# Layer 1: latent products and gates ahead of the spatial gating, whose products run ahead of group 2's state-space input product

## The chip, the cores and the metric

The kernel runs on one core of a Trainium2 chip. The metric is the time of one execution on the device in microseconds (us); lower is better. The kernel before takes 1910.93 us (median of three runs, 1908.58 to 1912.76).

The core's engines work side by side, each through its own queue in order: PE (TensorE, matrix products), DVE (VectorE), ACT (ScalarE), POOL (GpSimd), and SP, which issues the DMAs here.

## The reference

A two-layer block over 512 latent tokens and 256 context tokens of width 1024. In each layer the normalised, modulated input h goes through one input projection that is split into four mixers; their outputs are joined, projected and added; then comes a feed-forward with a convolution. Cut to what matters here:

```
def layer(x, c):                          # x: 512 latent tokens, c: 256 context tokens
    h = rmsnorm(x) * (1 + scale) + shift  # both streams
    p = h @ w_in                          # columns for A, B, C, D
    A: u, v = split(gelu(p_A));  v = rmsnorm(v) by heads;  out = u * (w_sp @ v + b_sp)
    B: q, k, v, r, gl = split(p_B); gate = cumsum(log_sigmoid(gl @ w_gate + b) / 16)
       out = rmsnorm(chunked gated linear attention(q, k, v, gate)) * silu(r)
    C: out = s5(p_C)                      # u -> complex state scan, both directions -> y
       y = gelu(y);  out = y * sigmoid(y @ w_glu + b_glu)
    D: latent attention on rmsnorm(p_D[:224]) (q) and rmsnorm(p_D[224:320]) (k, v), rotary
    x = x + gate * rmsnorm(concat(A, B, C, D) @ w_out)
    x = x + gate * rmsnorm(conv_ffn(rmsnorm(x) * ...))
```

In layer 1, the last, the context stream is read but not written: the outputs are the latent tokens.

## The kernel before

Tokens are worked in three groups of 256: groups 0 and 1 are the latent tokens, group 2 the context. h lies in SBUF as high and low parts (hhx and hlx for groups 0 and 1, hh2 and hl2 for group 2), and each weight tile, 128 x 1024, is loaded (`raw`, 512 KB, four buffers) and split into whi (ACT, L191) and wlo (DVE, L192), three buffers each. A product takes three matmuls for each of eight slices: `mm3` (L199, L200, L201).

The order on each engine is not written out: the scheduler of the tile framework simulates the program (`schedule_with_timeline_sim=True`) and lays down a fixed order from the order in which the code opens tiles and from its own times; pools and their tags (PSUM banks above all) decide what must wait for what. PSUM tags that matter: `pf` (six banks of the feed-forward, which stays open into the norm that ends a layer), `pn` (norms), `pg` (two banks for the mixers' input products), `pc1` (S5), `pb2` (one buffer, two banks) and `pb1` (mixer B, mixer A and the latent norms).

The place of the change is the passage from layer 0 to layer 1. At the end of layer 0's feed-forward a norm chain runs for each group: squares on ACT and DVE, sums by PE (`sums`, L322), root on DVE and POOL (L124, L125), broadcast by PE (`bcast`, L145), and `modulate`, which writes hh and hl by ACT, DVE and POOL (L385 to L391). Woven into it run the units of layer 1's S5 input product: `c_units` returns four units for groups 0 and 1, and two late units for group 2, which share the two weight tiles; each ends in a copy from PSUM to `rawm` (L1228). Then `mixers` runs for layer 1:

- `mixer_c` (S5): it transposes rawm into `s5a` (L696) and `s5u` (L703), multiplies by E (L714), copies into the state `s5v` (DVE L722 for one direction, ACT L724 for the other), and scans on DVE: seven steps over 12 blocks, eleven steps from block to block (L735, L737, L738 each), and a correction of all blocks (L753, L760, L762, L763). The states are copied to H (ACT L776, DVE L774), multiplied (L786, L788), put through gelu (L792), transposed (L798), gated (L814, L816 to L818) and stored.
- products ua and va of mixer A (in `pg`; ua has 48 matmuls of 512 columns, va 96 of 256), then `mixer_a`: squares and norm of va (L990, L991, L995), the spatial product (L1001, in `pb2`), L1003 and L1005, whose result `ut` is stored to DRAM.
- products cq and ck of mixer D, and the first part of `mixer_b`, the gates of four heads, in two pairs: L845 (PE, in `pb2`), L848 (ACT, Abs) and L849 (DVE); then for each pair Exp and Ln (ACT, L851, L852, each with a table load); then L855, L856 (a scan), L858, L859, L860 on DVE; last `dec` (DVE L866, L867 and ACT L868).
- `latent_norms`: squares (ACT L1037), sums (PE L1039, in `pb1`), root, broadcast (L145, in `pb2`), L1054 on DVE.
- product q (evacuated into tile `x12`, where `ut` and va were; L1536), its scaling L873 and L874, product vb (L1623), then k (L1536), r and the rest of `mixer_b` and `mixer_d`.

The scheduler merges these strands, so on PE the S5 instructions stand among the products.

Of the kernel before, what the change touches and what calls it, by code (L numbers as in the profile page):

```python
# [14 lines left out]
AF = mybir.ActivationFunctionType  # L15
ALU = mybir.AluOpType
AX = mybir.AxisListType
PSUM = bass.MemoryType.PSUM
# [4 lines left out]
T = NX + NCX  # L23
# [67 lines left out]
class Net:  # L91
# [1218 lines left out]
    def run(self, out):  # L1310
# [77 lines left out]
        for l in range(L):  # L1388
            ctx = l < L - 1
            G = (0, 1, 2) if ctx else (0, 1)  # L1390
            tn = T if ctx else NX
            self.mixers(l, ctx, md, (psls, tabs, tables) if l == 0 else None)
            with self.pool("f") as fp, self.pool("psf", space=PSUM) as psp:
# [43 lines left out]
                with ExitStack() as ye:  # L1437
# [60 lines left out]
                    if ctx:  # L1498
                        uf = [self.t(self.wp, [128, D], "rawm", bufs=2)[:, :T] for _ in range(2)]
                        self.uf[l + 1] = uf  # L1500
                        cu, late = self.c_units(l + 1, uf, psp)
                        self.weave(WV[4], down[1], c[:1])
                        self.weave(WV[5], down[2] + cu[:2], c[:2])
                        self.weave(WV[6], cu[2:], c[1:])
                        self.weave("", late, [])
                    else:
                        self.weave(WV[7], down[1], c)
            xsrc = xd
        es.close()

    def mixers(self, l, ctx, md, early=None):
# [9 lines left out]
        def fm(wv, groups):  # L1521
            px = pc = None
            if 0 in groups:
                px = self.t(self.psg, [128, 512], "pg")
                self.gemm_fm(wv, KT, self.hrhs, px, None, [g for g in groups if g < 2])
            if 2 in groups:
                pc = self.t(self.psg, [128, 512], "pg")
                self.gemm_fm(wv, KT, self.hrhs, None, pc[:, :256], [2])
            return px, pc


        def half(n, i):
            return self.wsplit(l, ("in", n), i)
# [6 lines left out]
        def tmajor(name, groups, sink):  # L1540
            wvs = [half(name, q) for q in range(2)]
            for g in groups:
                ps = self.t(self.psg, [128, 512], "pg")
# [9 lines left out]

        psls, tabs, tables = early or (self.pool("psb", space=PSUM), None, None)
# [5 lines left out]
        self.psg = psgs.__enter__()  # L1560
        mxs = self.pool("mx")
        px_ = mxs.__enter__()
        env = SimpleNamespace()
# [10 lines left out]
        rest = iter(())  # L1574

        def visit(n):
            for _ in range(n):
                next(rest, None)

        with self.pool("mc") as pm:  # L1580
# [7 lines left out]
            x12 = self.t(px_, [128, 4, T], "x12")  # L1588
            x6 = self.t(px_, [128, 1536], "x6")
            ut = x12[:, 0:2]  # L1590
            va = x12[:, 2:4].rearrange("p a t -> p (a t)").rearrange("p (i c) -> p i c", i=6)
            for i in range(2):
                px, pc = fm(half("ua", i), G)
                evac(ut[:, i], px, pc, func=AF.Gelu_apprx_tanh)
                visit(1)
            tmajor("va", G, lambda g, ps: nc.scalar.activation(
                va[:, 2 * g:2 * g + 2].rearrange("p i c -> p (i c)"), ps[:], AF.Gelu_apprx_tanh))
# [5 lines left out]
            for i in range(2):  # L1603
                px, pc = fm(half("cq", i), G3 if i else G)
                evac(cq[:, i], px, pc)
                visit(1)
            px, pc = fm(half("ck", 0), G3)
            evac(ck, px, pc)
            visit(2)
            if tabs:  # L1610
                tabs.__exit__(None, None, None)
            mgs = self.pool("mg", side="right")
            pg = mgs.__enter__()
            b = self.mixer_b(l, env, cq[:, 1], pg, ("pb2", "pb1"), ctx)
            next(b)
# [191 lines left out]
```

## Time and profile before

| | |
|---|---|
| median of three runs | 1910.93 us (1908.58 to 1912.76) |
| the profiled execution | 1912.24 us; its span 1910.4 us |
| PE busy | 1775.8 us, 93% of the span |
| DVE, ACT, POOL busy | 1197.7 us (63%), 776.7 us (41%), 123.9 us (6%) |
| TensorE's granted clock, mean | 0.944 of 2.4 GHz |
| chain that ended last | PE 71%, DVE 11%, issue 9%, ACT 4%, DMA 2% |

Busy time is that of one execution, taken by the hardware profiler; ends of matmuls are modelled, so for the rate of products the distance between two starts is read, not the length of one. The names L12 are lines of the kernel before. An idle time in brackets is the time that the engine waited ahead of an instruction, with the instruction that let it go on. The rows are in a section of their own below.

### The profile page before, as it was taken

The numbers are of one execution on the slowest core, as the hardware profiler recorded it, in microseconds if no ns is written. First come the engines' busy times: TensorE is split into PE (matmuls) and PEld (weight loads), VectorE is DVE, ScalarE is ACT, GpSimd is POOL, SyncE is SP. The second block draws the span as 40 slices with busy tenths as digits, with TensorE's granted clock in tenths as the row PEclk, the third lists the DMA queues.
The fourth block names the chain that finished last, engine by engine and source line by source line (L and its number), as shares of the span: only waits on it lengthen the run. The fifth ranks groups of instructions, "written<-read, shape, count | busy, mean of one in ns | idle before, by whom it ended". The sixth has DMA issues, their size and how long they took to land.

```text
span 1910.4 us, 28205 instructions
## 1 busy us (share of the span) xinstructions
PE 1775.8 (93%) x11256; PEld 1515.4 (79%) x11256; DVE 1197.7 (63%) x2200; ACT 776.7 (41%) x1242; POOL 123.9 (6%) x142
## 2 busy tenths in 40 slices
PE   5899989899989899999999988997989999999996
PEld 2785677679977788888888886886668988888886
DVE  8866734664879853554885775683565765455555
ACT  2433454454753333322322344364444653333332
POOL 0000000000430000000000033000000310000002
PEclk7999998899999999999999988998889899999998
DMA  9457630015623342222564433323102523323341
GB/s 351 140 170 253 200 95 24 28 37 185 204 70 112 109 122 78 88 89 85 183 185 133 143 100 104 115 69 95 33 24 94 187 83 88 110 78 110 86 146 45
DMA packets 94386, 222.14 MB, mean 116 GB/s; under 512 B 10928, under 2 KB 41008, under 8 KB 93232
## 3 DMA queue, kind: packets, MB, share of 16 engines
q1 hardware_dynamic: 94256, 220.36, 37.0%
q8 instruction: 88, 1.44, 0.3%
q14 instruction: 42, 0.34, 0.1%
HBM read 193.35 MB, written 24.08 MB: 114 GB/s over the span
## 4 chain that ended last, share of the span: by engine, by line
PE 71%; DVE 11%; issue 9%; ACT 4%; DMA 2%; POOL 1%; SPq 0%; POOLq 0%; DVEq 0%; ACTq 0%
PE pf L199 16%; PE pf L200 16%; PE pf L201 16%; PE pg L199 3%; PE pg L201 3%; PE pg L200 3%; PE pb L243 1%; DVE wlo L192 1%; PE pd L1161 1%; PE pn L322 1%; DVE z L1215 1%; PE pc L714 1%; ACT whi L191 1%; DMA bk<-bk 1%; DVE nu L389 1%
## 5 line engine op out<-in xcount | busy, mean ns | idle before, releaser
L192 DVE TENSOR_TENSOR wlo<-raw,whi 128x1024 fp32r<-128x1024 f32 (+1 forms) x215 | 252.5, 1175 | 292.4 <-ACT whi L191 289.5
L191 ACT ACTIVATE whi<-raw 128x1024 fp32r<-128x1024 f32 (+1 forms) x215 | 217.4, 1011 | 398.0 <-PE pf L200 340.7
L199 PE MATMUL pf<-hhx,whi 128*128 128x512 f32 (+1 forms) x1032 | 365.8, 360 | 13.3 <-DVE z L1215 6.0
L200 PE MATMUL pf<-hlx,whi 128*128 128x512 f32 (+1 forms) x1032 | 369.1, 359 | 6.1 <-DVE hlx L391 5.9
L201 PE MATMUL pf<-hhx,wlo 128*128 128x512 f32 (+1 forms) x1032 | 366.8, 357 | 0.7 <-DVE wlo L192 0.5
L199 PEld LDWEIGHTS pf<-hhx,whi 128*128 128x128 f32 x1032 | 199.9, 196 | 41.2 <-issue 7.3
L200 PEld LDWEIGHTS pf<-hlx,whi 128*128 128x128 f32 x1032 | 201.8, 196 | 33.6 <-DVE hlx L391 8.9
L201 PEld LDWEIGHTS pf<-hhx,wlo 128*128 128x128 f32 x1032 | 201.8, 196 | 27.0 <-DVE wlo L192 1.5
L199 PE MATMUL pf<-g,whi 128*128 128x512 f32 (+1 forms) x552 | 185.8, 342 | 5.3 <-DVE z L1215 2.9
L201 PE MATMUL pf<-g,wlo 128*128 128x512 f32 (+1 forms) x552 | 187.5, 341 | 0.8 <-DVE wlo L192 0.8
L200 PE MATMUL pf<-g,whi 128*128 128x512 f32 (+1 forms) x552 | 187.8, 341 | 0.0
L1215 DVE SCALAR_TENSOR_TENSOR z<-pf,cols,z 128x511 f32<-128x511 f32 (+1 forms) x264 | 167.9, 656 | 28.3 <-ACT z L1213 25.8
L200 PE MATMUL pf<-hl,whi 128*128 128x256 f32 x432 | 123.0, 286 | 0.4 <-DVE hl L391 0.4
L199 PE MATMUL pf<-hh,whi 128*128 128x256 f32 x432 | 121.5, 286 | 1.6 <-ACT hh L390 1.5
L201 PE MATMUL pf<-hh,wlo 128*128 128x256 f32 x432 | 122.1, 284 | 0.0
L199 PEld LDWEIGHTS pf<-g,whi 128*128 128x128 f32 x552 | 104.7, 192 | 18.8 <-issue 3.7
L201 PEld LDWEIGHTS pf<-g,wlo 128*128 128x128 f32 x552 | 105.8, 192 | 12.2 <-DVE wlo L192 1.0
L200 PEld LDWEIGHTS pf<-g,whi 128*128 128x128 f32 x552 | 105.8, 192 | 11.5 <-DVE g L1265 0.2
L1213 ACT ACTIVATE z<-pf,cols 128x512 f32<-128x512 f32 (+1 forms) x132 | 90.1, 695 | 38.3 <-PE pf L201 29.9
L1294 DVE TENSOR_TENSOR y<-y,pf 128x512 f32<-128x512 f32 (+1 forms) x88 | 44.7, 515 | 73.1 <-PE pf L201 73.1
L125 POOL TENSOR_TENSOR nroy<-nroy,mhalf 128x2 f32<-128x2 f32 x10 | 10.0, 996 | 1202.4 <-DVE nroy L124 894.3
L199 PEld LDWEIGHTS pf<-hh,whi 128*128 128x128 f32 x432 | 82.4, 193 | 3.9 <-ACT hh L390 2.3
(465 smaller groups left out, 3408.5 us busy)
## 6 DMA issues: line engine op xcount, KB each, us to landing
raw<-in_w SPq DMA_DIRECT2D x170, 512.0 KB, 3.5
rawm<-in_wmod SPq DMA_DIRECT2D x64, 512.0 KB, 4.3
raw<-in_w SPq DMA_DIRECT2D x48, 384.0 KB, 3.2
wm<-in_wmod SPq DMA_DIRECT2D x8, 1024.0 KB, 10.4
silu<-in_wmod SPq DMA_DIRECT2D x16, 512.0 KB, 5.6
dx<-g SPq DMA_DIRECT2D x32, 256.0 KB, 2.3
dG<-gt SPq DMA_DIRECT2D x16, 256.0 KB, 2.8
dE<-es SPq DMA_DIRECT2D x16, 256.0 KB, 2.3
```

Of the source, the lines that this page charges most:

```text
L191: nc.scalar.activation(hv, src, AF.Copy)
L192: nc.vector.tensor_tensor(lv, src, hv.bitcast(F32), op=ALU.subtract)
L199: self.nc.tensor.matmul(out, lh, rh, start=i == 0, stop=False)
L200: self.nc.tensor.matmul(out, lh, rl, start=False, stop=False)
L201: self.nc.tensor.matmul(out, ll, rh, start=False, stop=i == n - 1)
L243: self.nc.tensor.matmul(acc[32 * q:32 * q + 2, :], self.ct[:, k, :], halves[q // 2][:, q % 2 * 512:q % 2 * 512 + 512], start=k == 0, stop= ...
L322: self.nc.tensor.matmul(ps[:, j:j + 1], acc[:, k, j * 128:(j + 1) * 128], self.ones[:, 0:1], start=k == 0, stop=k == 1)
L389: nc.vector.scalar_tensor_tensor(u[:], xk, sc, pb, op0=ALU.mult, op1=ALU.mult)
L714: nc.tensor.matmul(ps[:, g * NCH:(g + 1) * NCH], E[:, b * 4 + g, :], U[:, gg, :], start=True, stop=True)
L1213: nc.scalar.activation(z[:, o:o + m], p[:, :m], AF.Identity, bias=b, scale=w1)
L1215: self.last = nc.vector.scalar_tensor_tensor(z[:, o + d:o + d + m - 1], p[:, s:s + m - 1], w, z[:, o + d:o + d + m - 1], op0=ALU.mult, op1 ...
L1294: nc.vector.tensor_tensor(y[:, m, t0:t0 + tw], y[:, m, t0:t0 + tw], ps[:, :tw], op=ALU.add)
```

## The change

Three things are moved, in layer 1 alone. The feed-forward's PSUM pool now stays open past the end of layer 0, and `mixers` gets it with the late units. First, products va and ua run in `pf` banks ahead of the late units (group 2's S5 input product). Second, `c_units` is called twice, once for the four early units and once for the two late ones, so that the late ones load and split the two weight tiles again. Third, `latents` (products cq and ck, and mixer_b's first part) comes ahead of `mixer_a`. In layer 0 all stands in the old order.

```diff
@@ run
+            if l == 0:
+                self.mixers(l, ctx, md, early=(psls, tabs, tables))
+            else:
+                self.mixers(l, ctx, md, late=(psf, psp, late))
+            psf = self.pool("psf", space=PSUM)
+            psp = psf.__enter__()
+            with self.pool("f") as fp:
...
-                        cu, late = self.c_units(l + 1, uf, psp)
+                        cu = self.c_units(l + 1, uf, psp)[0]
+                        late = self.c_units(l + 1, uf, psp)[1]
                         self.weave(WV[6], cu[2:], c[1:])
-                        self.weave("", late, [])
@@ mixers
+        def va_product():
+            tmajor("va", G, lambda g, ps: nc.scalar.activation(
+                va[:, 2 * g:2 * g + 2].rearrange("p i c -> p (i c)"), ps[:], AF.Gelu_apprx_tanh))
+        def ua_product():
+            for i in range(2):
+                px, pc = fm(half("ua", i), G)
+                evac(ut[:, i], px, pc, func=AF.Gelu_apprx_tanh)
+                visit(1)
+        if late:
+            psf, psp, units = late
+            self.psg = psp, "pf"
+            va_product()
+            ua_product()
+            for u in units:
+                u()
+            psf.__exit__(None, None, None)
...
+            def latents():
+                for i in range(2):
+                    px, pc = fm(half("cq", i), G3 if i else G)
+                    evac(cq[:, i], px, pc)
+                    visit(1)
+                px, pc = fm(half("ck", 0), G3)
+                evac(ck, px, pc)
+                visit(2)
+                if tabs:
+                    tabs.__exit__(None, None, None)
+                mgs = self.pool("mg", side="right")
+                pg = mgs.__enter__()
+                b = self.mixer_b(l, env, cq[:, 1], pg, ("pb2", "pb1"), ctx)
+                next(b)
+                return mgs, pg, b
+            if l:
+                mgs, pg, b = latents()
+            if not late:
+                ua_product()
+                va_product()
             visit(2)
             self.mixer_a(l, ut, va, x6, px_, "pb2", ctx)
             visit(2)
             for k in range(2):
                 store(0, k, ut[:, k])
+            if l == 0:
+                mgs, pg, b = latents()
```

The lists below show what stands in a row on an engine. PE at the end of layer 0's last norm, before (tile pf: products of the S5 input; pg: the first of ua's; hhx and hlx: groups 0 and 1, hh_1528 and hl_1529: group 2):

```order
L201 MATMUL pf_10525<-hhx_3543,wlo_10409 128x256
L322 MATMUL pn_10595<-ones_70,nsa_10563 128x1 x4
L145 MATMUL pn_10595<-cst_68,nry_10600 128x128 x2
L199 MATMUL pf_10647<-hh_1528_10605,whi_10376 128x256
L199 MATMUL pf_10673<-hh_1528_10605,whi_10408 128x256
...
L201 MATMUL pf_10673<-hh_1528_10605,wlo_10409 128x256
L696 MATMUL pc_1553_10750<-cst_68,rawm_9958 96x128
...
L696 MATMUL pc_1554_10756<-cst_68,rawm_9959 96x128
L199 MATMUL pg_11093<-hhx_3543,whi_11089 128x512
```

The same place now (pf_10672 and pf_10722: va; pf_10778 and pf_10810: ua; pf_10842 and pf_10874: group 2's S5 input; pg_11281: cq):

```order
L201 MATMUL pf_10672<-whi_10662,hlx_3544 128x256
L322 MATMUL pn_10595<-ones_70,nsa_10563 128x1 x4
L199 MATMUL pf_10672<-whi_10668,hhx_3543 128x256
...
L145 MATMUL pn_10595<-cst_68,nry_10600 128x128 x2
...
L199 MATMUL pf_10778<-hhx_3543,whi_10774 128x512
...
L201 MATMUL pf_10810<-hhx_3543,wlo_10807 128x512
L199 MATMUL pf_10842<-hh_1528_10605,whi_10838 128x256
...
L201 MATMUL pf_10874<-hh_1528_10605,wlo_10871 128x256
L696 MATMUL pc_1577_10940<-cst_68,rawm_9958 96x128
...
L696 MATMUL pc_1578_10946<-cst_68,rawm_9959 96x128
L199 MATMUL pg_11281<-hhx_3543,whi_11277 128x512
```

All 96 matmuls of va and 48 of ua stand ahead of group 2's product, and so ahead of the first transposes L696; behind these stand cq's instead of ua's.

DVE some steps into the scan of S5, before (L735, L737 and L738 on tiles s5a and s5v are a step; L1003 and L1005 are mixer_a's):

```order
L735 TENSOR_TENSOR s5a_10875<-s5l_10729,s5v_10723 128x768
L737 TENSOR_TENSOR s5v_10723<-s5v_10723,s5a_10875 128x12x32
L738 TENSOR_TENSOR s5v_10723<-s5v_10723,s5a_10875 128x12x32
L1003 SCALAR_TENSOR_TENSOR x_1596_11086<-pb_1615_11274,cols_9_80,x_1596_11086 128x512
L735 TENSOR_TENSOR s5a_10875<-s5l_10729,s5v_10723 128x768
L1005 TENSOR_TENSOR x_1595_11085<-x_1596_11086,x_1595_11085 128x512
L737 TENSOR_TENSOR s5v_10723<-s5v_10723,s5a_10875 128x12x32
L738 TENSOR_TENSOR s5v_10723<-s5v_10723,s5a_10875 128x12x32
```

DVE in the same steps now:

```order
L856 SCALAR_TENSOR_TENSOR bg_11431<-brs_11428,bsc_11432 128x768 x2
L735 TENSOR_TENSOR s5a_11065<-s5l_10919,s5v_10913 128x768
L858 COPY btot_11433<-bg_11431 128x12
L859 TENSOR_TENSOR bsc_11432<-bsc_11432,bg_11431 64x768
L858 COPY btot_11433<-bg_11431 128x12
L859 TENSOR_TENSOR bsc_11432<-bsc_11432,bg_11431 64x768
L192 TENSOR_TENSOR wlo_11815<-raw_11812,whi_11814 128x1024
L737 TENSOR_TENSOR s5v_10913<-s5v_10913,s5a_11065 128x12x32
L860 TENSOR_TENSOR bg_11431<-bsc_11432,btot_11433 64x768 x2
L738 TENSOR_TENSOR s5v_10913<-s5v_10913,s5a_11065 128x12x32
L849 TENSOR_SCALAR bsc_11432<-pb_1640_11456,cols_9_80 128x768
```

Where two of mixer_a's instructions and a step alternated, the gates of mixer_b (L856 to L860, L849) now stand between the instructions of one step.

PE around mixer_a's products (L1001) and mixer_b's last gate product (L845), before; all other rows here are products of cq, q and vb, in pg:

```order
L1001 MATMUL pb_1615_11274<-x_1596_11086,x_1595_11085 64x128 x8
L199 MATMUL pg_11361<-hh_1528_10605,whi_11332 128x256
...
L845 MATMUL pb_1636_11457<-cq_10706,wg_11449 128x512
L845 MATMUL pb_1636_11457<-cq_10706,wg_11449 128x256
L199 MATMUL pg_11557<-hhx_3543,whi_11553 128x512
...
L199 MATMUL pg_11743<-whi_11633,hh_1528_10605 128x256
L845 MATMUL pb_1639_11484<-cq_10706,wg_11449 128x512
L845 MATMUL pb_1639_11484<-cq_10706,wg_11449 128x256
L200 MATMUL pg_11743<-wlo_11634,hh_1528_10605 128x256
```

The same instructions now:

```order
L201 MATMUL pg_11604<-hhx_3543,wlo_11601 128x512
L845 MATMUL pb_1641_11461<-cq_10653,wg_11426 128x512
L845 MATMUL pb_1641_11461<-cq_10653,wg_11426 128x256
L1001 MATMUL pb_1645_11495<-x_1545_10659,x_1544_10658 64x128 x8
L1001 MATMUL pb_1646_11506<-x_1545_10659,x_1544_10658 64x128 x8
L1039 MATMUL pb_1647_11519<-ones_70,bsc_11520 128x1 x10
L199 MATMUL pg_11655<-whi_11645,hhx_3543 128x256
L200 MATMUL pg_11655<-wlo_11646,hhx_3543 128x256
```

Products stood between these small ones before; now the last L845, both L1001 and ten of L1039 stand in a row, and vb's product (pg_11655) behind them. L1039 stood behind the S5 output product L788 before.

## Rows read from the trace of the kernel before

**Rows 1.** The page, part 4: the chain that ended last, by engine.
```profile
PE 71%; DVE 11%; issue 9%; ACT 4%; DMA 2%; POOL 1%; SPq 0%; POOLq 0%; DVEq 0%; ACTq 0%
```

**Rows 2.** Windows by stage. Columns: stretch, length, busy us by engine, granted clock, DMA share, GB/s.
```profile
1148.37:1178.63 30.26, 21.08 (x109) 18.47 (x109) 19.36 (x37) 17.55 (x36) 15.62 (x20) 0.74 0.30 96
1178.63:1215.16 36.53, 36.52 (x256) 33.80 (x257) 14.28 (x28) 13.71 (x30) 1.71 (x1) 1.00 0.47 140
1215.16:1280.06 64.90, 64.49 (x388) 54.31 (x387) 56.27 (x91) 28.05 (x31) 1.19 (x1) 1.00 0.27 79
1280.06:1320.02 39.96, 28.26 (x176) 25.02 (x174) 21.05 (x37) 25.68 (x37) 2.27 (x1) 0.83 0.26 78
```

**Rows 3.** Timeline of PE ahead of T0: start, busy, instruction, idle before and its releaser.
```profile
1162.09 1.83 PE L322 MATMUL pn<-ones,nsa 128*128 128x1 f32 x8 [3.40 <-DVE nsa L311]
1168.61 0.41 PE L201 MATMUL pf<-hh,wlo 128*128 128x256 f32 x1
1168.82 0.41 PE L200 MATMUL pf<-hl,whi 128*128 128x256 f32 x1
1178.63 1.00 PE L696 MATMUL pc<-cst,rawm 128*96 128x128 f32 x7 [0.87 <-ACT rawm L1228]
```

**Rows 4.** Timeline of DVE: the scan's first step and its last.
```profile
1215.16 0.96 DVE L735 TENSOR_TENSOR s5a<-s5l,s5v 128x768 f32<-128x768 f32 x1 [1.79 <-ACT s5v L724]
...
1278.81 1.25 DVE L763 TENSOR_TENSOR s5v<-s5v,s5a 128x1056 f32<-128x1056 f32 x1
```

**Rows 5.** Windows of tile pg's work: 256-column products alone, then 512-column ones alone.
```profile
1254.58:1264.92 10.34, 10.34 (x86) 10.34 (x87) 1.75 (x3) 1.00 0.29 78
1229.96:1234.56 4.60, 4.60 (x21) 3.79 (x21) 0.00 (x0) 1.00 0.54 171
```

**Rows 6.** Windows from T0 to V: tile pg (products), then tile pc (S5).
```profile
1178.63:1215.16 36.53, 28.83 (x161) 23.91 (x162) 2.35 (x4) 1.00 0.47 140
1178.63:1215.16 36.53, 11.76 (x95) 11.16 (x95) 7.04 (x20) 6.36 (x20) 1.00 0.47 140
```

**Rows 7.** Windows from T0 to the last of k's first half: line L845 alone.
```profile
1178.63:1281.40 102.77, 6.21 (x16) 2.65 (x16) 1.00 0.35 103
```

**Rows 8.** Windows of one tile: s5v (the scan), then bsc (mixer_b and norms) in two stretches.
```profile
1215.16:1280.06 64.90, 0.00 (x0) 0.00 (x0) 32.75 (x64) 0.00 (x0) 1.00 0.27 79
1215.16:1280.06 64.90, 0.00 (x0) 0.00 (x0) 13.30 (x13) 0.00 (x0) 1.00 0.27 79
1280.06:1320.02 39.96, 3.40 (x28) 3.36 (x28) 11.55 (x12) 6.14 (x9) 0.83 0.26 78
```

**Rows 9.** Lines by form, DVE, 1215 to 1281: count, busy us, mean ns, idle before.
```profile
L192 DVE TENSOR_TENSOR wlo<-raw,whi 128x1024 fp32r<-128x1024 f32 x7 | 8.5, 1220 | 2.9 <-ACT whi L191 2.9
L849 DVE TENSOR_SCALAR bsc<-pb,cols 128x768 f32<-128x768 f32 x4 | 4.1, 1016 | 0.5 <-ACT bg L848 0.4
L1003 DVE SCALAR_TENSOR_TENSOR x<-pb,cols,x 128x512 f32<-128x512 f32 x2 | 1.5, 749 | 0.8 <-PE pb L1001 0.8
L1005 DVE TENSOR_TENSOR x<-x,x 128x512 f32<-128x512 f32 x2 | 1.4, 684 | 0.0
```

**Rows 10.** Windows from E to K2: line L1054 alone.
```profile
1280.06:1320.02 39.96, 2.05 (x3) 0.83 0.26 78
```

**Rows 11.** Timeline of ACT: a gate's Abs, the table load and Exp.
```profile
1247.41 0.90 ACT L848 ACTIVATE bg<-pb,cols 128x768 f32<-128x768 f32 x1 [0.69 <-PE pb L845]
1248.33 1.28 ACT L851 ACT_TABLE_LOAD   x1
1249.62 1.49 ACT L851 ACTIVATE bg<-bg 128x1536 f32<-128x1536 f32 x1
```

**Rows 12.** PE behind E: timeline, and lines by form of L1039.
```profile
1283.43 1.40 PE L788 MATMUL pc<-s5e,s5a 128*96 128x128 f32 x6 [2.09 <-ACT s5a L776]
...
1320.02 0.50 PE L199 MATMUL pg<-hhx,whi 128*128 128x512 f32 x1 [1.25 <-ACT bk L1536]
L1039 PE MATMUL pb<-ones,bsc 96*128 96x1 f32 x20 | 2.5, 247 | 1.1 <-ACT bsc L1037 1.1
```

More of the change, by code (lines that the diff above doesn't have):

```diff
@@ L1391, in run @@
             tn = T if ctx else NX
-            self.mixers(l, ctx, md, (psls, tabs, tables) if l == 0 else None)
-            with self.pool("f") as fp, self.pool("psf", space=PSUM) as psp:
+            if l == 0:
[5 more added lines that the diff above has]
+            with self.pool("f") as fp:
                 with self.pool("n1") as np_, self.pool("y1") as yp:
@@ L1508, in run, with mixers @@
             xsrc = xd
+        psf.__exit__(None, None, None)
         es.close()
-    def mixers(self, l, ctx, md, early=None):
+    def mixers(self, l, ctx, md, early=None, late=None):
         nc = self.nc
@@ L1523, in fm @@
             if 0 in groups:
-                px = self.t(self.psg, [128, 512], "pg")
+                px = self.t(self.psg[0], [128, 512], self.psg[1])
                 self.gemm_fm(wv, KT, self.hrhs, px, None, [g for g in groups if g < 2])
             if 2 in groups:
-                pc = self.t(self.psg, [128, 512], "pg")
+                pc = self.t(self.psg[0], [128, 512], self.psg[1])
                 self.gemm_fm(wv, KT, self.hrhs, None, pc[:, :256], [2])
@@ L1542, in tmajor @@
             for g in groups:
-                ps = self.t(self.psg, [128, 512], "pg")
+                ps = self.t(self.psg[0], [128, 512], self.psg[1])
                 for j in range(2):
@@ L1552, in store, with visit @@
             nc.sync.dma_start(md[:, o + k, t0:tn], mix[:, t0:tn])
+        rest = iter(())
+        def visit(n):
+            for _ in range(n):
+                next(rest, None)
+        mxs = self.pool("mx")
+        px_ = mxs.__enter__()
+        env = SimpleNamespace()
+        x12 = self.t(px_, [128, 4, T], "x12")
+        x6 = self.t(px_, [128, 1536], "x6")
+        ut = x12[:, 0:2]
+        va = x12[:, 2:4].rearrange("p a t -> p (a t)").rearrange("p (i c) -> p i c", i=6)
+        def va_product():
[13 more added lines that the diff above has]
+                u()
+            psf.__exit__(None, None, None)
         psls, tabs, tables = early or (self.pool("psb", space=PSUM), None, None)
@@ L1559, in mixers @@
         psgs = self.pool("psg", space=PSUM)
[L1560 to L1563, printed above, removed]
+        self.psg = psgs.__enter__(), "pg"
         def heads(n, x, groups):
@@ L1572, in heads @@
                     nc.sync.dma_start(x[64 - hr * 64:128 - hr * 64, 2 * hp + hr, :w], x[rs, 2 * hp + hr, :w])
[L1574 to L1578, printed above, removed]
         with self.pool("mc") as pm:
@@ L1587, in mixers @@
             visit(2)
[L1588 to L1597, printed above, removed]
+            def latents():
[18 more added lines that the diff above has]
+                va_product()
             visit(2)
@@ L1602, in mixers @@
                 store(0, k, ut[:, k])
[L1603 to L1615, printed above, removed]
+            if l == 0:
+                mgs, pg, b = latents()
             visit(2)
```

## The prediction

> **What bounds the kernel now.** I read the page first: PE carries 71% of the chain that ended last [rows 1]. So the first question of every edit is whether it removes PE idle time or makes some. An average does not answer that, so I cut the place of the change into stages at the points of layer 1's state-space mixer (S5), since its scan runs on DVE, alone, for longer than any other piece here. The cuts are T0, the first transpose of the scan's input (L696), 1178.63; V, the first scan step on DVE (L735), 1215.16; E, the end of the last scan step (L763), 1280.06; and K2, where PE starts the second half of the k product, 1320.02, behind which the order of both kernels is alike [rows 2, 3, 4, 12].
>
> The stage table shows what a reader must see: before T0 PE works 21.08 of 30.26 us at a granted clock of 0.74; from T0 to E it works 101.0 of 101.4 us at 1.00; from E to K2 28.26 of 39.96 us [rows 2]. It looks as if PE bounds the middle. But PE's product work ends just when the scan does (the first output product L788 then waits 2.09 us, for ACT's copies of the scan's result, [rows 12]), so T0 to E is two paths of the same length: PE's queue, and the chain transposes, V, DVE scan, E. The work that the change takes out of this stretch is the cover of that chain.
>
> **The change, part by part.** (Layer 0's order does not change; I put it at 0.)
>
> 1. *T0.* ua and va products move ahead of group 2's state-space product, and so ahead of T0. That is 48 matmuls of 512 columns and 96 of 256. At full clock a 512 takes 4.60/21 = 0.22 us and a 256 takes 10.34/86 = 0.12 us [rows 5], so 10.5 + 11.5 = 22.0 us go in front of T0. What do they fill? The idle 9.2 us of the first stage, of which the wait for DVE's sum of squares (3.40) is the largest piece [rows 3], and its slow clock: two neighbouring matmuls of 256 start 0.21 us apart there instead of 0.12 [rows 3]. With everything packed and fast, group 1's and group 2's products are 96 x 0.12 = 11.5, L322, L145 and waits for L1228 about 2.8; with 22.0 that is 36.3 us after 1148.4: T0 at 1184.7, 6 us later. With nothing refunded but the idle time, 21.1 + 22.0 = 43.1, and some 3 us left of waiting: 1194.5, 16 us later. The second call also reloads group 2's two weight tiles and splits them again: two whi on ACT, two wlo on DVE of 1.22 [rows 9], in the middle of the group-2 norm, where ACT and DVE also work for hh and hl. I take 1189: **+10.5** (bounds +6, +16).
>
> 2. *T0 to V.* In this stretch 161 product matmuls stood beside S5's own 95 [rows 6]: 48 + 96 of ua and va (22.0 us) and 17 x 0.22 = 3.7 us of cq, which leaves 10.8 us of the 36.5 to the 95. In their place now stand cq, ck and the start of q: 91 x 0.22 + 48 x 0.12 = 25.7 us, and two of mixer_b's gate products (L845), 6.21/4 = 1.55 us each [rows 7]. 10.8 + 25.7 + 3.1 = 39.6. Then ACT: the second gate's Abs (0.90), an activation table load (1.28) and Exp (1.49) [rows 11] now stand ahead of the last eight copies to V, for which V waited 1.79 us before [rows 4]: 3.7 more, and about 1 for the queue behind them. So 44.5 instead of 36.5: **+8** (bounds +4, +11).
>
> 3. *V to E.* DVE's queue goes in order. Of the 64.9 us, 32.75 are the scan's own instructions [rows 8] and 56.27 - 32.75 = 23.5 are others among them [rows 2, 8]. After the change nearly all of mixer_b's gating, mixer_a's ends, the latent norms and q's scaling stand among the scan's steps: all work on bsc, 13.30 + 11.55 = 24.85 in the two windows, less the two L849 that now come before V (2 x 1.02) [rows 8, 9]; L1003 and L1005, 2.9, and two weight splits, 2.4 [rows 9]; the three L1054, 2.05 [rows 10]; small copies some 2. That is 32.2 us, so 65 us of DVE work. Before, 8.6 us of the stretch were waits; I leave 5 (Ln of the second pair of gates comes after two table loads), so 70: **+5** (bounds 0, +9).
>
> 4. *E to K2.* L1039's matmuls and their wait are now gone from here: 2.5 us for 20 of the 28, so 3.5 for all, and 1.1 of wait [rows 12]. Part of it lay in waits of S5's output chain: **-3.5** (bounds -7, 0).
>
> 5. *PE's queue meanwhile.* The fourth gate product needs the only pb2 buffer, which the third L849 frees; that stands 16 us of DVE work behind V. Then mixer_a's two products (L1001) pass through the same buffer, L1039 waits for the norms' squares, which stand on ACT behind the dec of all gates, and vb's product needs a pg bank that is freed by q's evacuation, which overwrites ut and so waits until DVE's last L1005 and its store are done, some 41 us of DVE work behind V. I count PE idle for about 12 us ahead of the fourth L845 and 15 to 20 us ahead of vb. Then 144 x 0.12 + 24 x 0.22 + 12 x 0.12 = 24 us of products follow, which end at about 1309, where L788 (E = 1303.5, plus the 3.4 us as before) would be free too. So both paths end together and this part costs **0** extra; without the scan's delay it would be the bound itself.
>
> Sum: 10.5 + 8 + 5 - 3.5 = **+20 us**. The profiled execution took 1912.24 us, 1.3 above the median of the runs; added to the median, 1910.93 + 20 = **1931 us**. By the ends of the terms (+3, +36; by halves of each, since they don't all fall one way) this case's own range is 1922 to 1939.
>
> **Rivals.**
>
> *PE bound, refund in full (faster).* If the scan is not what ends last (its delays absorbed, V earlier than I have it), only PE's sum counts. The first stage is 30.26 us for work that needs 11.5 + 2.8 = 14.3 at full clock, so 16 us come back: 1895 us. For it: PE is 99.6% busy from T0 to E [rows 2]; the products that fill the first stage need nothing from the norm. Against: L788 waited for the scan already, and 22 us of cover are gone while the work beside the scan on DVE grows.
>
> *Only T0 moves (slower, small).* If DVE's added work fits its 8.6 us of waits and ACT's order costs V nothing, then 101.4 us follow T0 as before and the output phase is 3.5 shorter: +7, 1918 us. This case decides from the point at which others' work among the scan steps stays under about 27 us.
>
> *No change.* T0 at its lower end (+6) and the output phase at its lower end (-7) cancel: 1910 us.
>
> *A cold PE behind the new gaps (slower still).* PE starts vb after 15 to 20 us with little work. The granted clock was 0.74 in the stage with such waits before T0 and 0.83 from E to K2, and 1.00 where PE never waited [rows 2]; a 256 at the lower of the two levels (1.2 GHz) is 0.21 us apart instead of 0.12 [rows 3, 5]. If all of vb's 144 ran so, 144 x 0.09 = 13 us would come on top: +33, 1944 us. The Trainium skill, "TensorE: Matmul & The Clock Gate", section "HAM oscillation — how this bites in real kernels", says that a TensorE that waits between its bursts is throttled again and starts the next burst slowly. It speaks for the change ahead of T0 and against it at vb; the stage table bears it out in both.
>
> **How the numbers follow.** Chances: the forecast 0.60; only T0 moves (or between +4 and +11 by another mixture) 0.14; within 0.2% 0.07; the refund, whole or in part, 0.12; the cold PE 0.07. A measurement of this kernel can tell about 0.2%, 3.8 us, from no change; so faster 0.12, same 0.07, slower 0.81. The range leaves out the refund (0.12) and the upper half of the last rival (0.04), and a little more: 1908 to 1943.
>
> **What would show it.** In the profile of the changed kernel: the stage before T0 denser and at a higher clock, T0 near 1189 (1178.63 before); two more raw loads and splits; V some 44 us later; L849, L855, L856, L874 and L1054 among the scan's steps, and E some 70 us behind V; PE idle ahead of the fourth L845, released by DVE L849, and ahead of vb, released by ACT's q evacuation; L1039 gone from behind E; K2 near 1340. It would be wrong if K2 came before 1320, that is, if V to E stayed near 60 us and T0 moved under 6; if PE was not idle between V and E; or if the stages behind K2, which I hold equal, differ by more than 3 us.

## The result and the profile after

The changed kernel takes 1935.75 us (median of four runs, 1932.31 to 1937.40), the kernel before 1911.85 us in the same comparison. The ratio is 1.0118, with a 95% interval of 1.0095 to 1.014: 22.6 us slower (18 to 27). The forecast was 1931 us, +20, with a range of 1908 to 1943.

The profiled execution took 1937.40 us, with a span of 1935.6. Its page, engines and the chain that ended last:

```profile
PE 1782.9 (92%) x11256; PEld 1519.2 (78%) x11256; DVE 1200.0 (62%) x2202; ACT 780.3 (40%) x1244; POOL 124.7 (6%) x142
...
PE 72%; DVE 10%; issue 9%; ACT 4%; DMA 2%; POOL 1%; SPq 0%; POOLq 0%; DVEq 0%; ACTq 0%
```

PE is busy 7.1 us longer than before and the span is 25.2 us longer, so most of the loss is idle time of PE. The stages of [rows 2] in the changed kernel, cut at the same four points (the first from the group-1 product to T0, then T0 to V, V to E, E to K2; columns as in [rows 2]):

```profile
1153.94:1195.23 41.29, 37.51 (x254) 34.70 (x254) 28.55 (x47) 26.71 (x48) 19.06 (x21) 0.97 0.46 141
1195.23:1239.15 43.92, 43.92 (x259) 37.35 (x260) 13.69 (x26) 16.37 (x33) 0.00 (x0) 1.00 0.41 124
1239.15:1307.88 68.73, 40.52 (x252) 35.92 (x251) 62.45 (x108) 24.18 (x29) 2.64 (x1) 0.73 0.12 34
1307.88:1344.79 36.91, 26.86 (x165) 21.77 (x163) 9.54 (x15) 19.44 (x27) 0.00 (x0) 0.91 0.35 100
```

The points themselves: the first transposes L696 on PE (T0), then on DVE the second gate's L849 and the first scan step (V), the last scan step (E is its end), the first output product L788, and the second half of the k product (K2); they answer to [rows 3, 4, 12]:

```profile
1195.23 1.00 PE L696 MATMUL pc<-cst,rawm 128*96 128x128 f32 x7 [1.18 <-ACT rawm L1228]
...
1234.16 1.02 DVE L849 TENSOR_SCALAR bsc<-pb,cols 128x768 f32<-128x768 f32 x1 [6.37 <-ACT bg L848]
1239.15 0.96 DVE L735 TENSOR_TENSOR s5a<-s5l,s5v 128x768 f32<-128x768 f32 x1 [3.97 <-ACT s5v L724]
...
1306.63 1.25 DVE L763 TENSOR_TENSOR s5v<-s5v,s5a 128x1056 f32<-128x1056 f32 x1
...
1314.28 0.60 PE L788 MATMUL pc<-s5e,s5a 128*96 128x128 f32 x4
...
1344.79 0.50 PE L199 MATMUL pg<-hhx,whi 128*128 128x512 f32 x1 [2.14 <-ACT bk L1542]
```

**Where the time went.** T0 is 16.6 us later than before, but 5.5 of these are not the change's. They are there before the change begins: the first convolution of layer 0's feed-forward, whose order is the same in both kernels, starts at 542.27 us before and at 547.76 after. The lag arises around 250 us, where the same instructions met another granted clock. The kernel before (timeline of ACT, then windows of all engines):

```profile
542.27 1.45 ACT L1213 ACTIVATE z<-pf,cols 128x512 f32<-128x512 f32 x2 [1.22 <-PE pf L201]
...
240.00:250.00 10.00, 10.00 (x76) 9.81 (x77) 2.40 (x11) 8.58 (x11) 1.40 (x1) 0.83 0.19 55
250.00:260.00 10.00, 10.00 (x53) 8.08 (x52) 5.92 (x7) 7.18 (x11) 0.87 (x1) 1.00 0.19 54
```

The changed kernel, the same instruction and the same windows:

```profile
547.76 1.45 ACT L1213 ACTIVATE z<-pf,cols 128x512 f32<-128x512 f32 x2 [1.22 <-PE pf L201]
...
240.00:250.00 10.00, 10.00 (x56) 10.00 (x57) 1.83 (x7) 6.51 (x8) 0.00 (x0) 0.57 0.11 24
250.00:260.00 10.00, 10.00 (x45) 8.62 (x46) 5.46 (x9) 8.15 (x11) 2.27 (x1) 0.75 0.26 82
```

So each stage is measured from that convolution, f0, below. With it the change costs 11.1 us at T0, 7.4 more at V, 3.8 more at E, gives 3.0 back up to K2, and the two kernels then run alike: 19.7 of the 25.2 us arise behind f0 and are put down to the change.

Between V and E the scan now shares DVE with mixer_b. One scan step of the changed kernel, on DVE:

```profile
1245.30 3.40 DVE L856 TENSOR_TENSOR_SCAN bg<-brs,bsc 128x768 f32<-128x768 f32 x2
1248.62 0.94 DVE L735 TENSOR_TENSOR s5a<-s5l,s5v 128x768 f32<-128x768 f32 x1
1249.65 0.96 DVE L859 TENSOR_TENSOR bsc<-bsc,bg 64x768 f32<-64x768 f32 x1
1250.82 0.95 DVE L859 TENSOR_TENSOR bsc<-bsc,bg 64x768 f32<-64x768 f32 x1
1251.81 1.23 DVE L192 TENSOR_TENSOR wlo<-raw,whi 128x1024 fp32r<-128x1024 f32 x1
1252.95 0.55 DVE L737 TENSOR_TENSOR s5v<-s5v,s5a 128x384 f32<-128x384 f32 x1
1253.53 1.82 DVE L860 TENSOR_TENSOR bg<-bsc,btot 64x768 f32<-64x768 f32 x2
1255.39 0.56 DVE L738 TENSOR_TENSOR s5v<-s5v,s5a 128x384 f32<-128x384 f32 x1
1255.86 1.01 DVE L849 TENSOR_SCALAR bsc<-pb,cols 128x768 f32<-128x768 f32 x1
```

Between L735 at 1248.62 and its L737 at 1252.95 stand gate steps and a weight split, and L860 then keeps L738 for two more. DVE is busy 62.45 of 68.73 us there; before it was 56.27 of 64.90.

PE meanwhile is idle for 28.2 of the 68.73 us. Its waits in that stretch, by what ended them (total us, times, longest):

```profile
PE pb L845 <- DVE bsc L849: 12.7, 1, 12.7
PE pb L1039 <- ACT bsc L1037: 8.5, 1, 8.5
PE pb L1001 <- DVE x L1003: 4.9, 1, 4.9
PE pb L1001 <- DVE bsc L849: 2.2, 1, 2.2
```

The granted clock there is 0.73: it reads 1.00 up to 1244, 0.50 (1.2 GHz) while the small products between the waits run, and 1.00 again from 1289.4 on. Four L845 take 1.55 us before the long wait and 2.89 behind it. vb's product begins at the lower level and rises within 4 us: neighbours of 256 columns stand 0.21 us apart and then 0.12:

```profile
1239.88 1.55 PE L845 MATMUL pb<-cq,wg 32*128 32x512 f32 x4
...
1257.02 2.89 PE L845 MATMUL pb<-cq,wg 32*128 32x512 f32 x4 [12.66 <-DVE bsc L849]
...
1288.44 0.41 PE L200 MATMUL pg<-wlo,hhx 128*128 128x256 f32 x1
1288.65 0.41 PE L201 MATMUL pg<-whi,hlx 128*128 128x256 f32 x1
...
1289.40 0.28 PE L199 MATMUL pg<-whi,hhx 128*128 128x256 f32 x1
1289.52 0.28 PE L200 MATMUL pg<-wlo,hhx 128*128 128x256 f32 x1
```

### The profile page after: what moved, and what is told of

The parts are those of the page before. It is cut to its first block, busy times and chain, and to the rows that moved or that the text cites. A ratio compares the mean times of both kernels' runs of the same rounds, so it can differ in the third digit from the quotient of the medians.

```text
span 1935.6 us, 28214 instructions
## 1 busy us (share of the span) xinstructions
PE 1782.9 (92%) x11256; PEld 1519.2 (78%) x11256; DVE 1200.0 (62%) x2202; ACT 780.3 (40%) x1244; POOL 124.7 (6%) x142
## 4 chain that ended last, share of the span: by engine, by line
PE 72%; DVE 10%; issue 9%; ACT 4%; DMA 2%; POOL 1%; SPq 0%; POOLq 0%; DVEq 0%; ACTq 0%
PE pf L199 17%; PE pf L200 17%; PE pf L201 16%; PE pg L199 3%; PE pg L201 3%; PE pg L200 3%; DVE wlo L192 1%; PE pb L243 1%; PE pd L1161 1%; PE pn L322 1%; ACT whi L191 1%; DVE z L1215 1%; DVE nu L389 1%; PE pb L845 1%; PE pb L1039 1%
## 5 line engine op out<-in xcount | busy, mean ns | idle before, releaser
L199 PE MATMUL pf<-hhx,whi 128*128 128x512 f32 (+1 forms) x1048 | 370.7, 359 | 13.1 <-DVE z L1215 5.8
L200 PE MATMUL pf<-hlx,whi 128*128 128x512 f32 (+1 forms) x1048 | 374.5, 358 | 5.5 <-DVE hlx L391 5.4
L201 PE MATMUL pf<-hhx,wlo 128*128 128x512 f32 (+1 forms) x1048 | 372.3, 357 | 0.5 <-DVE wlo L192 0.5
L201 PEld LDWEIGHTS pf<-g,wlo 128*128 128x128 f32 x552 | 105.8, 192 | 12.2 <-DVE wlo L192 1.0
L200 PEld LDWEIGHTS pf<-hl,whi 128*128 128x128 f32 x432 | 82.6, 191 | 2.0 <-DVE hl L391 0.4
```

The lines of the kernel that those rows point to most:

```text
L199: self.nc.tensor.matmul(out, lh, rh, start=i == 0, stop=False)
L200: self.nc.tensor.matmul(out, lh, rl, start=False, stop=False)
L201: self.nc.tensor.matmul(out, ll, rh, start=False, stop=i == n - 1)
```

## The experiments

Theory: the chain T0, V, E and the S5 output sets the end; products ahead of T0 delay its start, other work of DVE among the scan's steps lengthens it, and PE's idle time is a result, not a cause. Rivals: PE's waits for pb2 and q's evacuation are the cause; or the second load and split of the weights is what delays T0.

All stages of the profiled executions in one table, in us. T0 is given from f0 against the kernel before (636.4 us from f0); S is the end of the last gating product L814, since k's second half has another place in some kernels; the first L885 is mixer B's first transpose of k, which needs all gates; "ratio" is that of the timed runs with its interval.

| kernel | T0 | T0 to V | V to E | E to S | S to first L885 | ratio to before |
|---|---|---|---|---|---|---|
| before | 0 | 36.5 | 64.9 | 37.8 | 11.8 | 1 |
| changed | +11.1 | 43.9 | 68.7 | 34.8 | 11.1 | 1.0118 (1.0095 to 1.014) |
| products only | +11.1 | 39.3 | 69.3 | 34.3 | 12.2 | 1.0042 (1.0021 to 1.0062) |
| latents only | -4.0 | 43.9 | 76.0 | 31.9 | 11.0 | 1.0028 (1.0003 to 1.0053) |
| reload only | +3.5 | 38.1 | 64.9 | 37.5 | 12.3 | 1.0012 (0.9994 to 1.0031) |
| q in its own tile | +12.0 | 43.9 | 71.0 | 32.8 | 11.4 | 1.0088 (1.0055 to 1.0122) |
| late units first | +15.8 | 44.0 | 71.4 | 33.4 | 10.9 | 1.0149 (1.0122 to 1.0176) |
| products, scan first | +11.0 | 39.3 | 45.6 | 41.3 | 19.7 | 1.001 (0.9993 to 1.0026) |
| before, scan first | -0.2 | 38.1 | 51.0 | 42.5 | 20.5 | 0.9949 (0.9931 to 0.9967) |
| changed, scan first | +8.6 | 43.9 | 37.7 | 35.4 | 39.2 | 1.0049 (1.003 to 1.0069) |
| second pair behind | -0.1 | 38.1 | 64.9 | 37.9 | 11.9 | 1.0004 (0.9987 to 1.0021) |

Single executions of one program differ: in the first of these comparisons the kernel before ran from 1907.90 to 1922.14 us in 25 runs. T0 from f0 varies too: latents only and the kernel before have the same order up to T0 and differ by 4.0 us. Stages between T0 and S repeat better: T0 to V reads 43.9 or 44.0 in the five kernels with cq, ck and gates there. In the kernel before it reads 36.5, though, and 38.1 in three kernels with its order in that stretch, so of the change's +7.4 at V some 1.6 may be that execution's.

**Products only** (the diff is against the changed kernel):

```diff
-            if l:
-                mgs, pg, b = latents()
...
-            if l == 0:
-                mgs, pg, b = latents()
+            mgs, pg, b = latents()
```

> Only the products va and ua stand ahead of group 2's S5 input product (with its second load of the weights); cq, ck and the gates stand behind mixer A as before. Theory (the S5 chain T0, V, E, K2 sets the end, and other work on DVE among the scan steps lengthens it): T0 11 us later than before, T0 to V about 39 us, V to E about 69 (65 us of DVE work, as many gate steps among the scan as in the changed kernel), E to K2 about 36.5; sum +14 us, 1926. Rival 1 (the waits of PE for pb2 and for q's evacuation made the loss, not the scan): these are gone here, so at most T0's 11 us remain, 1915 to 1923. Rival 2 (refund of the first stage): 1896.

Measured: 1920.32 us, ratio 1.0042, some +8 (4 to 12). Windows T0 to V and V to E, and the last gating products, which end at S, 1337.95:

```profile
1194.98:1234.28 39.30, 39.30 (x259) 34.14 (x260) 15.57 (x30) 12.79 (x29) 0.00 (x0) 1.00 0.43 140
1234.28:1303.61 69.33, 51.62 (x290) 44.84 (x288) 61.99 (x105) 30.04 (x34) 2.64 (x1) 0.82 0.20 57
...
1331.90 6.05 PE L814 MATMUL pc<-s5u,s5e 128*128 128x512 f32 x8
```

T0, T0 to V and V to E came as the theory had them (+11.1, 39.3 and 69.3 against +11, 39 and 69). The output did too: L1039 and L145 stand ahead of L788 here, and E to S is 34.3 us instead of 37.8, 3.5 less. From f0 the stages make +14.9 up to S, where the theory had +14 up to K2, and this execution, the slowest of the ten, ends 12.5 us later than before. The timed runs say less, +8: below the theory's 1926 and inside the range of the first rival, which gave no figures for the stages. PE waits only 0.7 us ahead of L845 here instead of 12.7, and V to E is as long, so that wait does not make the stretch long. PE still waits 8.9 us ahead of L1039 and 7.5 ahead of L145, so PE's waits as such are not ruled out by this run.

**Latents only** (against the changed kernel):

```diff
-                self.mixers(l, ctx, md, late=(psf, psp, late))
+                psf.__exit__(None, None, None)
+                self.mixers(l, ctx, md)
...
-                        cu = self.c_units(l + 1, uf, psp)[0]
-                        late = self.c_units(l + 1, uf, psp)[1]
+                        cu, late = self.c_units(l + 1, uf, psp)
...
+                        self.weave("", late, [])
```

> Only cq, ck and the gates stand ahead of mixer A; ua and va stand behind group 2's product in pg, weights loaded once. Theory (S5 chain): T0 as before, T0 to V 44 us (+8), V to E some 80 us (76 us of DVE work, 59 before), E to K2 36.5 (-3.5): +19 us, 1931. Rival (PE's waits made the loss): ua's and va's 22 us of products fill PE's gaps between the gate products, so within 4 us of before, 1912.

Measured: 1922.90 us, ratio 1.0028, +5 (1 to 10). Windows T0 to V, V to E, E to S:

```profile
1178.43:1222.35 43.92, 43.92 (x259) 37.35 (x260) 13.69 (x26) 16.37 (x33) 0.00 (x0) 1.00 0.39 117
1222.35:1298.33 75.98, 66.46 (x414) 59.61 (x413) 71.08 (x117) 34.08 (x41) 5.40 (x2) 0.89 0.22 67
1298.33:1330.21 31.88, 24.24 (x145) 19.87 (x143) 5.90 (x12) 15.75 (x20) 0.00 (x0) 0.84 0.31 90
```

Here PE has its cover: it is busy for 66.46 of the 75.98 us from V to E, and the stretch is still 11 us longer than before, since DVE is busy for 71.08 of it. The lengthening of this stretch comes from DVE and not from PE's waits. The +19 expected did not come: T0 fell 4 us early in this execution, and E to S gave back 5.9, not 3.5, which leaves +8.5 at S and +8.9 at the end, from f0; the timed +5 is smaller still, and its interval holds the rival's 4. The two parts alone make some +8 and +5 in the timed runs, less than the whole's +23. In the profiled executions, from f0 to S, they make +14.9 and +8.5, the whole +19.3, so the stages do not show the parts to be cheaper than the whole.

**Reload only** (against the kernel before):

```diff
-                        cu, late = self.c_units(l + 1, uf, psp)
+                        cu = self.c_units(l + 1, uf, psp)[0]
+                        late = self.c_units(l + 1, uf, psp)[1]
```

> The kernel before with the second call of c_units alone: two more weight loads and splits, the order otherwise the same. Theory: 0 to +2 us at T0, so the same time, 1911 to 1914. Rival (the reload in the midst of the group-2 norm is what moves T0 by 11): +5 to +11.

Measured: 1916.83 us, ratio 1.0012 with an interval that holds 1. T0 is 3.5 us late in the profiled execution, which is inside what T0 varies by. The second load costs at most 6 us by the interval, not 11.

**Late units first** (against the changed kernel; the weights are loaded once):

```diff
-            va_product()
-            ua_product()
             for u in units:
                 u()
+            va_product()
+            ua_product()
...
-                        cu = self.c_units(l + 1, uf, psp)[0]
-                        late = self.c_units(l + 1, uf, psp)[1]
+                        cu, late = self.c_units(l + 1, uf, psp)
```

> The whole change, but with the late units written ahead of va and ua, which then share the two weight tiles of the early units (no second load). PE still does all of va and ua ahead of L696. Theory (T0 is late since 22 us of products stand ahead of it): T0 9 to 11 us later than before, the rest as in the changed kernel, 1929 to 1935. Rival (the second load and split hold up the group-2 norm): T0 only 4 to 6 us later, 1925 to 1929.

Measured: 1940.12 us, ratio 1.0149 (the profiled execution is a short one, with a span of 1926.6). T0 is +15.8, not earlier, without any second load: va and ua still stand ahead of L696. That ends the rival of the reload. The time is above the 1929 to 1935 expected. Why T0 is later still than in the changed kernel, the trace shows; PE ahead of group 2's product:

```profile
1154.55 1.83 PE L322 MATMUL pn<-ones,nsa 128*128 128x1 f32 x8 [3.40 <-DVE nsa L311]
...
1160.16 0.80 PE L199 MATMUL pf<-hh,whi 128*128 128x256 f32 x2 [1.52 <-ACT hh L390]
```

These are the norm's waits of the kernel before, 6.0 us with one of 1.0 ahead of L145. va and ua stand behind group 2's product here and cannot fill them; in the changed kernel va's matmuls stand there, and L322 and L145 do not wait. T0 is 4.7 us later than in the changed kernel.

**q in its own tile** (against the changed kernel; `Halves` gives q's four heads two tiles that the modulation no longer needs):

```diff
-            env.q = self.t(px_, [128, 4, T], "x12")
+            if l:
+                env.q = Halves([self.t(self.cp, [128, D], f"silu{w}") for w in range(2)])
+            else:
+                env.q = self.t(px_, [128, 4, T], "x12")
```

> The changed kernel, but q is evacuated into a tile of its own, so that vb's product no longer waits for mixer A's store; the scheduler then puts vb's 96 matmuls ahead of the fourth gate product. Theory (scan is the bound, PE merely ties): PE's idle of some 28 us between V and E shrinks by 15 or more, but E moves by 0 to +4 (69.5 us of DVE work among the scan steps against 65.8), so the time stays within 5 us of the changed kernel, 1931 to 1941. Rival (PE's waits made the loss): 10 us or more come back, 1925 or less.

Measured: 1931.39 us, ratio 1.0088, at the lower end of the theory's range; its interval overlaps that of the changed kernel, and the rival's 10 us did not come back. Windows V to E and E to S:

```profile
1233.89:1304.94 71.05, 48.77 (x298) 43.52 (x296) 66.03 (x110) 26.06 (x31) 4.71 (x1) 0.78 0.18 55
1304.94:1337.73 32.79, 21.75 (x116) 17.65 (x116) 4.43 (x10) 14.43 (x19) 0.00 (x0) 0.74 0.21 56
```

PE's idle time from V to E fell by 6 us only, to 22.3 (the scheduler moved vb, but L1039 still waits 8.9 us for its squares), so the test is weaker than it was meant to be. What it shows: 8 us more of PE's work stand in that stretch, and E came 2.3 us later behind V, with DVE busy for 66.03 of 71.05.

**Products, scan first.** The edge orders mixer_b's gate steps on DVE behind the scan's last step. Against products only (inside, the lines count one more: L857 there is L856 here):

```diff
-            tt(dst, dst, q, op=ALU.add)
+            self.scan = tt(dst, dst, q, op=ALU.add)
...
+            with self.behind(self.scan if l else None):
                 for h in (2 * hp, 2 * hp + 1):
```

> Only the products ahead of group 2's product, and in layer 1 mixer B's gate steps on DVE (L855 to L860) ordered behind the last scan step of S5. Theory (other DVE work among the scan steps is what makes V to E long): V to E falls from 69 to about 44 us (40 us of DVE work), T0 stays 11 us late, so E comes some 9 us earlier than in the kernel before; L1039 stands behind the output phase; the time is 1900 to 1906, 7 to 13 us under the kernel before. Rival 1 (PE's 99.6% from T0 to E bounds, the scan does not): no gain over the products alone, 1915 to 1923. Rival 2 (the gates, now late, become the bound behind the output phase): E early by 9 us, but the first L885 no earlier than before, 1911 to 1920.

Measured: 1916.50 us, ratio 1.001, no difference from before; the 1900 to 1906 expected did not come. Windows V to E, E to S, S to the first L885:

```profile
1233.52:1279.13 45.61, 39.19 (x246) 33.88 (x244) 39.23 (x71) 16.36 (x18) 0.00 (x0) 0.95 0.29 83
1279.13:1320.42 41.29, 29.38 (x140) 24.21 (x140) 25.34 (x37) 23.53 (x28) 0.00 (x0) 0.68 0.18 50
1320.42:1340.15 19.73, 14.92 (x79) 13.32 (x78) 8.64 (x16) 9.69 (x16) 2.82 (x1) 0.74 0.29 91
```

V to E fell by 23.7 us, from 69.3 to 45.6 (44 expected), and E comes 5.5 us before that of the kernel before. Of these 24 us some 6 reached the end (ratio 1.0042 and 1.001, by two comparisons): E to S grew by 7.0, and S to L885 by 7.6. The time lies in the ranges of both rivals. The first L885 comes 5.8 us later than before, as the second has it: the profile's chain to it runs over the late gate steps on DVE (to 1309.95) and then over L1039, L145 and 10 us of products on PE, so the gates alone do not set it.

**Before, scan first** (the same edge, by the same diff, in the kernel before):

> The kernel before with that order edge alone: the gate steps on DVE behind the last scan step. Theory: V to E falls from 64.9 to about 49 us (45 us of DVE work), T0 and V unchanged, the rest of k's products then fills the output phase; PE's idle of 11.7 us there goes, time 1898 to 1904. Rival 1 (PE bounds the stretch): PE's queue alone from T0 to k's end is 101 us, so at most 3 us, 1909 to 1913. Rival 2 (late gates): slower than before, 1915 or more.

Measured: 1904.44 us, ratio 0.9949 (0.9931 to 0.9967): 10 us faster than the kernel before, and the fastest of all. Windows T0 to V, V to E, E to S, S to L885:

```profile
1174.99:1213.13 38.14, 38.14 (x256) 35.01 (x257) 14.27 (x29) 13.81 (x30) 1.71 (x1) 0.96 0.47 134
1213.13:1264.17 51.04, 51.04 (x308) 42.84 (x307) 43.54 (x77) 19.11 (x23) 1.19 (x1) 1.00 0.30 87
1264.17:1306.69 42.52, 34.42 (x210) 27.70 (x208) 28.98 (x39) 27.65 (x32) 0.00 (x0) 0.88 0.30 85
1306.69:1327.14 20.45, 17.01 (x98) 15.25 (x97) 7.46 (x16) 9.69 (x16) 2.82 (x1) 0.75 0.29 88
```

V to E is 51.0 us (49 expected) with DVE busy for 43.54 of it, and PE is busy for all of it. From E to S PE now works 34.42 us instead of 27.37 before: k's products fill a part of the waits of the output (8.1 us of idle are left of 10.5). So a part of PE's 101 us could be moved behind E, and the first rival (PE bounds) falls. The way from there to the 10 us is not shown. From f0, E comes 12.4 us and S 7.7 us earlier than before, but the first L885 0.9 us later: L1039 and L145 now stand behind S, and the second pair's gate steps begin at 1293.92 instead of 1279.97. The profiled execution gains behind it, where L885 to the next feed-forward takes 212.2 us instead of 221.3, with 1621 and 1619 matmuls and 19.4 and 20.2 us of PE idle: PE is busy for 192.79 us instead of 201.08, at a granted clock of 0.92 instead of 0.88. That stretch reads 212 to 224 us in the eleven kernels, and no run shows what shortens it here.

**Changed, scan first** (the same edge, by the same diff, in the changed kernel):

> The changed kernel with the gate steps on DVE behind the last scan step; the scheduler then puts mixer A's products, vb's and k's behind the S5 output products. Theory: V to E falls from 69 to about 37 us (35 of DVE work), E some 9 us earlier than in the kernel before, but some 42 us of products (vb, k) now have no scan to run beside and come after the output phase: the first L885 some 5 to 12 us later than before, 1917 to 1925, and PE idle for 20 us or more between V and E. Rival (the scan's end alone sets the time): 1900 to 1905.

Measured: 1924.40 us, ratio 1.0049, as expected (the first L885 comes 13.8 us later than before, 5 to 12 expected). Windows V to E, E to S, S to L885:

```profile
1231.16:1268.87 37.71, 5.20 (x22) 3.17 (x20) 35.07 (x67) 5.67 (x5) 0.00 (x0) 0.63 0.10 29
1268.87:1304.26 35.39, 26.85 (x154) 21.74 (x154) 27.66 (x41) 23.29 (x28) 0.00 (x0) 0.77 0.25 73
1304.26:1343.45 39.19, 39.19 (x289) 37.28 (x289) 12.53 (x20) 17.14 (x27) 2.82 (x1) 1.00 0.34 100
```

This measures the scan by itself: with two weight splits and nothing else it takes 37.7 us. E comes 11.2 us earlier than before, S 13.6, and still the kernel is slower: PE worked 5.20 us in the scan, and the products that had run beside it follow behind, 39.2 us from S to L885. Against the changed kernel E is 33.5 us earlier from f0, and the timed runs gain some 13 (1.0118 and 1.0049): without products beside the scan, most of its early end is lost. So the scan's end alone does not set the time.

**Second pair behind** (the edge for the second pair of gates alone; against the kernel before with the edge):

```diff
-            with self.behind(self.scan if l else None):
+            with self.behind(self.scan if l and hp else None):
```

> The kernel before with the order edge for the second pair of gates alone; the first pair's steps stay among the scan's (57.6 us of DVE work from V to E against 59.1 before and 45.1 with the edge for both pairs). If the gain of the edge comes from the scan that ends earlier, as the theory has it: V to E some 62 us, E 3 us earlier, time 2 to 5 us under the kernel before. Rival (the gain comes from the second pair's place behind the scan): as large as with the edge for both pairs, 8 to 11 us under the kernel before.

Measured: 1912.73 us, ratio 1.0004: no difference. Window V to E:

```profile
1215.46:1280.35 64.89, 64.48 (x388) 54.30 (x387) 56.25 (x91) 28.04 (x31) 1.19 (x1) 1.00 0.28 79
```

The stretch is as long as before, and so is the time, because this edge moved nothing. The second pair's first step on DVE:

```profile
1280.27 1.82 DVE L856 TENSOR_TENSOR bsc<-bsc,bg 128x768 f32<-128x768 f32 x2
```

In the kernel before it starts at 1279.97, behind the scan's last step already, and from the scan's first step on DVE's rows stand in the same order in both kernels. So this run repeats the kernel before (the 57.6 us counted beforehand did not come: DVE is busy for 56.25 us, before for 56.27) and decides nothing between theory and rival. What the edge for both pairs takes out of V to E are mainly the first pair's steps.

## Why the prediction was right, point by point

1. *T0.* +10.5 was worked out, +11.1 measured from f0, and +11.0 to +12.0 in three more kernels with the same order up to there (+8.6 in one). The first stage is dense now: 37.51 of 41.29 us at 0.97, where it was 21.08 of 30.26 at 0.74, so about half of the 22 us of products was refunded by idle time and clock. That it would be half was a choice: the working gave the bounds, +6 and +16, and +10.5 lies in the middle, so the good fit of this term is in part luck.
2. *T0 to V.* 44.5 worked out, 43.9 measured, against 36.5 to 38.1 in the old order. The copies to V waited for Abs, the table load and Exp as read from the order: V waited 3.97 us for L724, 1.79 before.
3. *V to E.* 70 worked out, 68.7 measured; DVE was busy for 62.45 us, and I had 65. The seven kernels in which this stretch was counted beforehand gave 69.3, 76.0, 71.0, 45.6, 51.0, 37.7 and 64.9 for 69, 80, 69 to 73, 44, 49, 37 and 62: the count of DVE's work plus some 4 us of waits came within 4 us. The waits themselves are no constant: the stretch is 2.6 us (changed, scan first) to 8.6 us (before) longer than DVE is busy in it. In the kernel before and in before, scan first, PE is busy for the stretch too (64.49 of 64.90, 51.04 of 51.04), so there its length alone does not tell the two engines apart.
4. *E to K2.* -3.5 worked out, -3.0 measured. In products only, where L1039 and L145 also went ahead of L788, E to S fell by 3.5.
5. *PE's queue.* 12.7 us of idle ahead of the fourth L845, released by L849, 12 worked out. The wait that I put ahead of vb (15 to 20 us) came out at 15.6, but ahead of L1001 and L1039: vb itself didn't wait, since q's evacuation began at 1284.04 on ACT and vb at 1285.52. PE reached L788 at 1314.28, some 3 us later than E alone would have let it (E + 3.4 = 1311.3), so the two paths did not quite tie, and PE's was the longer: the profile's chain that ended last runs through L763 and ACT's L776 to L788 in the kernel before, but here from the gate steps on DVE through ACT's L1037, PE's L1039 at 1281.23 and the products behind it. So the scan's last step was not what L788 waited for. It cost little: E to S is 34.8 us here and 34.3 in products only, where L788 starts 3.3 us behind E.
6. *The sum.* The stages make +19.3 up to K2, the whole +19.7 from f0; the timed runs say 22.6 (18 to 27). That the profiled difference was 25.2 is the other granted clock in layer 0.

The rivals. The refund in full and no change fell with the time. Only T0 moving fell with V to E. The cold PE was there, but cheaper: vb ran at the lower level for 4 us, not for all of its 144 products, so 18 of them at 0.09 us, 1.6 us, where I had priced 13. What I had not priced are the small products in the gap: L845 took 2.89 us instead of 1.55, L1001 2.88 twice where the kernel before has 1.58, and eighteen L1039 3.98 instead of 2.07, some 6 us of PE's time in all. How much of that reached the end no run shows.

What the runs show is where each delay comes from: products ahead of T0 make it late without a second load, gates ahead of V make V late, and other work among the scan's steps makes V to E long. They do not show that the scan's chain alone sets the end: in the three kernels in which it ended early, 5.5 to 12.4 us before that of the kernel before, the first L885 came 0.9 to 13.8 us later. Two things stay open: why the two parts alone cost 8 and 5 us in the timed runs where the whole costs 23, and where the 10 us of before, scan first, come from.

## What to carry to other kernels

Count what stands on the engine of a dependent chain between its first and last step, others' work too: that sum plus 3 to 9 us was the length of the stretch in every kernel here. Work that only fills the chain's engine can be tried behind it. In timed runs this gave some 10, 6 and 13 us on three bases (before, products only, changed), where the stretch itself became 14, 24 and 31 us shorter: products that had run beside the chain, and the work put off, then stood behind it. Look whether an order edge moved anything before its run is read as a test. And before a difference of two profiles is read stage by stage, look for a stretch whose order did not change: its lag is not the change's.

## What was not expected of the hardware

The same instructions in the same order ran 5.5 us apart in layer 0 of two executions, where the granted clock was 0.57 and 0.75 in two windows of one and 0.83 and 1.00 in the other; 25 runs of the kernel before spread over 14 us. The Trainium skill, "TensorE: Matmul & The Clock Gate", section "HAM oscillation — how this bites in real kernels", tells of a clock that falls where TensorE waits; the trace agrees for V to E of the changed kernel (0.73 with 28.2 us of idle). There the price was 1.6 us on vb's products and some 6 us on the small products ahead of them.
